# Adding the sparse-attention mask on GpSimd instead of by a TensorE matmul, for five of eight soft-max heads

## The chip, the cores and the metric

The kernel runs on one core of one Trainium2 chip. The metric is the device time of one launch in microseconds (us). The kernel before takes 675.26 us (median of 3 runs, 674.33 to 675.56).

## What is computed

Two layers of an encoder, 512 frames wide 1024. Each layer has one input projection, two kinds of attention on its columns (eight heads each), a gate, an output projection and a layer norm. The change lies in group B, attention over the 128 keys that a cheap indexer picks for each query, with soft-max and a position bias:

```python
score = jnp.where(admissible[None], score, -jnp.inf)
vals, idx = lax.top_k(score, topk)
valid = vals > -jnp.inf
...
logits = jnp.einsum('bqhd,bqkhd->bqhk', qb, kg).astype(jnp.float32) * scale
bias = rel_bias[t5_bucket(idx - t[None, :, None])]
logits = logits + jnp.swapaxes(bias, -1, -2).astype(jnp.float32)
logits = jnp.where(valid[:, :, None, :], logits, -jnp.inf)
p = jax.nn.softmax(logits, axis=-1)
return jnp.einsum('bqhk,bqkhd->bqhd', p.astype(vg.dtype), vg)
```

The kernel gathers nothing. It computes all logits of a block of 128 queries against the keys up to the end of that block and adds a mask: 0 where the key was picked, -1e30 where it was not.

## The kernel before

**Slots.** A layer is a loop over 91 slots (`for s in range(SLOTS + 3)`, L713). Each slot starts one attention block of 128 queries and carries two older ones on. Slots 0 to 23 are the indexer, 24 to 55 the eight stick-breaking heads (class `Stick`), 56 to 87 the eight soft-max heads (class `Soft`, L585). A head is four blocks, `qb` 0 to 3, with n = 128, 256, 384 and 512 keys. Within its slot, a soft-max block does: `stage0` (scores z by TensorE into PSUM), `stage1` (VectorE: negated logits and their row minimum), `stage1b` (ScalarE: exponential and row sum). Two slots later the block is transposed (TensorE, L407) and evacuated (ScalarE L415, VectorE L418); when a head's last block is that far, and one slot more has gone by, `values` multiplies it with the values (TensorE, L556) and `mix` takes the result to M (ScalarE L464, VectorE L466, GpSimd L467).

**Matmul operands** are split in a high and a low part to reach float32 accuracy. So z is two matmuls (L399, L402). Between them stands the mask matmul of a soft-max block:

```python
T.matmul(self.z[:, :nn], a, b, start=True, stop=False)
if mask is not None:
    T.matmul(self.z[:, cols], identb, mask, start=False, stop=False, skip_group_check=True)
T.matmul(self.z[:, :nn], c, d, start=False, stop=True)
```

It multiplies the bf16 mask by a bf16 identity and accumulates it onto z. A stick-breaking block has the same two matmuls and no mask. L599 then adds the position bias: tile `gbias` (512 columns, read backwards), one per head, loaded by `Head.load` (L526) from a table in DRAM into a pool of three buffers.

**Order.** The four compute engines run in the order in which the code issues (`manual_schedule`, L112). The DMA queue of SyncE (SP) isn't in that list: the scheduler places its transfers itself. Between the attention steps of a slot, `fill` issues projection matmuls on TensorE (L221 to L223, L247 to L249) up to a count that the tables `A_PINS`, `B_PINS` and `P1` give for that slot. At the end of a slot, `prep_ahead` (L187) splits the next weight piece: ScalarE writes `whi` (L175) and GpSimd writes `wlo` in two halves of 512 columns (L177). Four `whi`/`wlo` pairs are held at a time.

**GpSimd in the soft-max slots** has the `wlo` splits (L177), one M multiplication per head (L467), one per pair of heads by the reciprocal sums, tile `over` (L550), and from slot 76 on the splits of M for the output projection (L145).

**Pools that the change touches**: `wk` (three buffers, the block tiles `p`, `om` and `relu`) and the two buffers of tile `over` in `tp`.

Of the kernel before, what the change touches and what calls it, by code (L numbers as in the profile page):

```python
# [11 lines left out]
F32 = mybir.dt.float32  # L12
# [3 lines left out]
ALU = mybir.AluOpType  # L16

P = 128
D = 1024
S = 512  # L20
# [11 lines left out]
SCALE = 1.0 / math.sqrt(HD)  # L32
# [59 lines left out]
def tile_hybrid(ctx: ExitStack, tc: tile.TileContext, xt, x, w_in, w_ki, w_out, ln_g, ln_b, rel_bias, onehot, out, depth=DEPTH):  # L92
    nc = tc.nc
    V, A, G, T = nc.vector, nc.scalar, nc.gpsimd, nc.tensor
# [5 lines left out]
    kp = ctx.enter_context(tc.tile_pool(name="kp", bufs=3))  # L100
    vp = ctx.enter_context(tc.tile_pool(name="vp", bufs=2))
    gp = ctx.enter_context(tc.tile_pool(name="gp", bufs=3))
    wk = ctx.enter_context(tc.tile_pool(name="wk", bufs=3))
    tp = ctx.enter_context(tc.tile_pool(name="tp", bufs=2))
    sm = ctx.enter_context(tc.tile_pool(name="sm", bufs=4))
    PS = bass.MemoryType.PSUM
# [12 lines left out]
    mask = [const.tile([P, P * (b + 1)], BF16, name=f"mask{b}") for b in range(NTB)]  # L119
# [89 lines left out]
    def flush():  # L209
        while later:  # L210
            later.pop(0)()
# [67 lines left out]
    def run_pending(at_once=False):  # L279
        for p in pending:  # L280
            p[0] -= 1
        while pending and (at_once or pending[0][0] < 0):
            pending.pop(0)[1]()
# [98 lines left out]
    def load_residual():  # L382
        for tb in range(NTB):
            nc.sync.dma_start(XN[:, tb], x[tb * P : (tb + 1) * P, :])
# [37 lines left out]
    def layer(l):  # L422
        last_layer = l == depth - 1
        st = {}
# [36 lines left out]
        def mix(pair, s, o, engine=G):  # L461
            hi, lo = (slice(0, 64), slice(64, 128)) if s == 0 else (slice(64, 128), slice(0, 64))
            t = tp.tile([P, S], F32, tag="t", name="mixt")
            A.activation(t[hi], o[lo], AF.Copy)  # L464
            if ("g", pair) in made:
                V.tensor_tensor(t[hi], o[hi], t[hi], ALU.add)  # L466
                engine.tensor_tensor(M[hi, pair, :], M[hi, pair, :], t[hi], ALU.mult)  # L467
            else:
                V.tensor_tensor(M[hi, pair, :], o[hi], t[hi], ALU.add)
            made.add(("o", pair, s))  # L470

        def mix_split(pairs, tbs, lo_engine=G):
            src = M[:, pairs, tbs.start * P : tbs.stop * P].rearrange("p m (a b) -> p m a b", b=P)
            hi, lo = (t[:, tbs, pairs, :].rearrange("p a m b -> p m a b") for t in (XH, XL))
            split(hi, lo, src, lo_engine=lo_engine)
# [14 lines left out]
        class Index(Block):  # L490
# [4 lines left out]
            def stage0(self):  # L495
                q = QKV["I", self.h // 4, "q"][self.h % 4 // 2]
                self.product(q, self.h % 2, st["ki"], 0, spare=(3 * self.h + self.qb) % 2 == 0)

            def stage1(self):
                self.r = wk.tile([P, S], F32, tag="w", name="relu")  # L500
                A.activation(self.r[:, : self.n], self.z[:, : self.n], AF.Relu, scale=absw[:, self.qb, self.h : self.h + 1])
# [13 lines left out]
        class Head:  # L515
# [20 lines left out]
            def spread(self):  # L536
                rec = over_sum[self.s]
                V.reciprocal(rec[:, :NTB], self.sums)
                turned = sm.tile([P, 32], F32, tag="turned", name="turned")
                V.transpose(turned, rec)  # L540
                if self.s == 0:
                    st["over"] = tp.tile([P, S], F32, tag="over", name="over")
                rows = r_dram[8 * l + 4 * self.i + self.hh]
                nc.sync.dma_start(rows.rearrange("c (b k) -> b c k", k=32), turned)
                over, pair = st["over"], self.pair
                back = bass.AP(tensor=rows.tensor, offset=rows.offset, ap=[[0, 64], [1, S]])
                part = over[64 * self.s : 64 * self.s + 64]
                pending.append([1, lambda: nc.sync.dma_start(part, back)])
                if self.s == 1:
                    pending.append([SUM_SLOTS, lambda: G.tensor_tensor(M[:, pair, :], M[:, pair, :], over, ALU.mult)])  # L550
# [34 lines left out]
        class Soft(Block):  # L585
            def __init__(self, head, qb):
                super().__init__(qb)
                self.head = head

            def stage0(self):  # L590
                if self.qb == 0:
                    self.head.load()
                self.product(*self.head.operands(), mask=mask[self.qb], cols=slice(0, self.n))

            def stage1(self):
                h, n, b = self.head, self.n, slice(self.qb, self.qb + 1)
                self.p = wk.tile([P, S], F32, tag="w", name="p")
                p = self.p[:, :n]
                V.tensor_tensor_reduce(out=p, in0=self.z[:, :n], in1=h.g[:, :n][:, ::-1], scale=-SCALE, scalar=3.0e38, op0=ALU.add, op1=ALU.min, accum_out=h.mn[:, b])  # L599

            def stage1b(self):
                h, b = self.head, slice(self.qb, self.qb + 1)
# [13 lines left out]
        tasks = [Index(h, qb) for h in range(IDX_HEADS) for qb in range(1, NTB)]  # L616
# [53 lines left out]
        def fill(s):  # L670
            while st["done"] < target(s) - 300:
                if st["gen"] is None:
                    if not queue:
                        return
                    st["gen"] = queue.pop(0)()
                step = next(st["gen"], None)
                if step is None:
                    st["gen"] = None
                else:
                    st["done"] += step  # L680
# [3 lines left out]
        def topk_rounds(upto):  # L684
            while rounds and 48 - len(rounds) < upto:
                qb = rounds.pop(0)
                m8 = sm.tile([P, 8], F32, tag=f"m8{qb}", name="m8", bufs=2)
                V.max(m8, scores[qb])  # L688
                V.match_replace(scores[qb], m8, scores[qb], TAKEN)  # L689
                if not rounds:  # L690
                    for b in range(1, NTB):
                        V.tensor_scalar(mask[b], scores[b], -2.0e38, MASKED, ALU.is_gt, ALU.mult)
# [17 lines left out]
        def at(t):  # L710
            return tasks[t] if 0 <= t < len(tasks) else None

        for s in range(SLOTS + 3):  # L713
            if s == IDX_SLOTS:
                tasks[s - 1].stage2()
                for step in range(PAUSE):
                    fill(s + (step + 1) / PAUSE)
                    flush()
                    topk_rounds(step + 1)
                    stream.prep_ahead()  # L720
            now = s + (s >= IDX_SLOTS)
            done, old = at(s - 3), at(s - 2)
            done = done if isinstance(done, (Stick, Soft)) and done.qb == NTB - 1 else None
            old = old if isinstance(old, (Stick, Soft)) else None
            if at(s):
                tasks[s].stage0()
            if at(s - 1) and s != IDX_SLOTS:
                tasks[s - 1].stage2()
            if at(s):
                tasks[s].stage1()  # L730
            flush()
            fill(now + FRAC[0])
            if old:
                old.transpose()
                old.evacuate(old.head.at)
            if isinstance(at(s), Soft):
                tasks[s].stage1b()
            if old:
                old.evacuate_lo(old.head.at)
            if s in SPLITS:  # L740
                tb = SPLITS.index(s)
                mix_split(slice(0, 6), slice(tb, tb + 1))
            if s == SPLIT6:
                mix_split(slice(6, 7), slice(0, NTB))
            if s >= IDX_SLOTS:
                topk_rounds(PAUSE + RATE * (s + 1 - IDX_SLOTS))
            fill(now + FRAC[1])
            run_pending()
            if done:
                done.head.values()  # L750
                last = s == SLOTS + 2
                mix(done.head.pair, done.head.s, done.head.o, V if last else G)
            fill(now + 1)
            stream.prep_ahead()
            if l == 0 and s == 1:
                load_residual()
                load_bias_table()
            if l == 0 and s in (6, 9):
                make_bias_table(s == 9)
            if s == 72:  # L760
                gb = kp.tile([P, 2, D], F32, tag="k", name="gb")
                for j, t in enumerate((ln_g, ln_b)):
                    row = t[l : l + 1, :]
                    nc.sync.dma_start(gb[:, j, :], bass.AP(tensor=row.tensor, offset=row.offset, ap=[[0, P], [1, D]]))
            if s == PREP[0]:
                stream.prep(index[l, "o"] + 2)
            if s == PREP[1]:
                stream.prep(index[l, "o"] + 3)
# [75 lines left out]
    for l in range(depth):  # L844
        layer(l)
# [49 lines left out]
```

## Time and profile before

| | before |
|---|---|
| Median of 3 runs | 675.26 us (674.33 to 675.56) |
| Profiled execution, its time | 674.73 us |
| Profiled execution, span | 672.9 us |
| TensorE (PE) busy | 659.6 us, 98% |
| PE weight loads (PEld) busy | 553.7 us, 82% |
| VectorE (DVE) busy | 482.7 us, 72% |
| ScalarE (ACT) busy | 351.5 us, 52% |
| GpSimd (POOL) busy | 330.6 us, 49% |
| Mean granted TensorE clock | 0.997 |

A time is some 1.8 us more than the span between the first and the last instruction. Busy times are the union of an engine's instructions. Matmuls overlap in the pipeline, so the duration of one is longer than what it takes from the engine: that is read from one start to the next. Some matmul records are missing from a trace.

### The profile page before, as it was taken

The page shows a single profiled execution, that of the slowest core. Times are in us where ns is not written, and L with a number is a line of the kernel's source. Part 1 is how long each engine was busy: PE and PEld are TensorE (multiplying, and loading weights), DVE is VectorE, ACT ScalarE, POOL GpSimd, SP SyncE. Part 2 cuts the span into 40 slices and gives each one's busy share as a digit, 9 for nine tenths or more (in the row PEclk, how much of TensorE's full clock was granted, in tenths as well). Part 3 has the DMA queues.
Part 4 walks back from the last instruction along what each step waited for, and adds up shares of the span by engine and source line. Part 5 has one row for each costly group of instructions (what it writes and reads, how often), then busy time and mean ns, then how long its engine had stood idle before and what let it go on. Part 6 is the DMA issues. An engine that isn't in the chain of part 4 may idle for free.

```text
span 672.9 us, 10299 instructions
## 1 busy us (share of the span) xinstructions
PE 659.6 (98%) x3575; PEld 553.7 (82%) x3589; DVE 482.7 (72%) x1019; ACT 351.5 (52%) x707; POOL 330.6 (49%) x303
## 2 busy tenths in 40 slices
PE   8999999999999999999999999999999999999995
PEld 4778988988889879877897888889888898897784
DVE  3588899999855455666853689999989554556576
ACT  4576545445447556773233765544534565568610
POOL 5343634466564433764354344445566533457531
PEclk9999999999999999999999999999999999999998
DMA  7625224242342354212125143432114534442022
GB/s 247 221 82 146 95 94 126 64 128 92 99 140 82 115 142 152 82 52 94 41 82 171 64 120 101 126 94 94 64 63 142 126 111 123 123 148 68 32 94 94
DMA packets 26203, 72.85 MB, mean 108 GB/s; under 512 B 5124, under 2 KB 6788, under 8 KB 26152
## 3 DMA queue, kind: packets, MB, share of 16 engines
q1 hardware_dynamic: 26152, 72.20, 34.4%
q8 instruction: 28, 0.46, 0.3%
q14 instruction: 23, 0.19, 0.1%
HBM read 58.87 MB, written 2.31 MB: 91 GB/s over the span
## 4 chain that ended last, share of the span: by engine, by line
PE 88%; DVE 5%; POOL 2%; DMA 2%; issue 1%; ACT 1%; SPq 1%; DVEq 0%; POOLq 0%; ACTq 0%
PE pj L221 14%; PE pj L222 14%; PE pj L223 14%; PE o L556 6%; PE tr L407 5%; PE z L402 4%; PE pjo L642 4%; PE pjo L644 4%; PE pjo L641 4%; PE z L399 4%; PE pjv L249 4%; PE pjv L248 4%; PE pjv L247 4%; POOL wlo L177 1%; DMA XN<-in_xt_dram 1%
## 5 line engine op out<-in xcount | busy, mean ns | idle before, releaser
L177 POOL TENSOR_TENSOR wlo<-raw,whi 128x512 fp32r<-128x512 f32 (+1 forms) x168 | 228.0, 1378 | 157.7 <-ACT whi L175 139.7
L221 PE MATMUL pj<-XH,whi 128*128 128x512 f32 (+1 forms) x456 | 185.4, 407 | 0.4 <-ACT whi L144 0.4
L222 PE MATMUL pj<-XL,whi 128*128 128x512 f32 (+1 forms) x456 | 178.9, 392 | 0.8 <-DVE XL L145 0.8
L223 PE MATMUL pj<-XH,wlo 128*128 128x512 f32 (+1 forms) x456 | 179.2, 393 | 0.0
L223 PEld LDWEIGHTS pj<-XH,wlo 128*128 128x128 f32 (+1 forms) x456 | 84.9, 186 | 20.3 <-POOL wlo L145 0.4
L175 ACT ACTIVATE whi<-raw 128x1024 fp32r<-128x1024 f32 (+1 forms) x87 | 91.2, 1050 | 19.9 <-PE pjo L642 6.6
L222 PEld LDWEIGHTS pj<-XL,whi 128*128 128x128 f32 (+1 forms) x456 | 85.4, 187 | 15.3 <-DVE XL L145 2.4
L221 PEld LDWEIGHTS pj<-XH,whi 128*128 128x128 f32 (+1 forms) x456 | 85.3, 187 | 15.1 <-ACT whi L144 1.1
L247 PE MATMUL pjv<-whi,XH 128*128 128x256 f32 x256 | 75.3, 294 | 0.0
L569 ACT ACTIVATE om<-z 128x128 f32<-128x128 f32 (+1 forms) x64 | 27.9, 437 | 86.9 <-PE z L402 80.7
L575 DVE TENSOR_TENSOR_SCAN om<-om 128x128 f32<-128x128 f32 (+1 forms) x64 | 69.3, 1082 | 5.1 <-POOL om L571 4.9
L249 PE MATMUL pjv<-wlo,XH 128*128 128x256 f32 x256 | 72.5, 283 | 0.3 <-POOL wlo L177 0.3
L248 PE MATMUL pjv<-whi,XL 128*128 128x256 f32 x256 | 72.2, 282 | 0.0
L467 POOL TENSOR_TENSOR M<-M,mixt 64x512 f32<-64x512 f32 x22 | 32.0, 1452 | 72.7 <-DVE mixt L466 39.3
L688 DVE MAX8 m<-scores 128x8 f32<-128x256 f32 (+2 forms) x96 | 52.8, 550 | 0.2
L689 DVE MATCH_REPLACE8 scores<-m,scores 128x256 f32<-128x256 f32 (+2 forms) x96 | 52.1, 542 | 0.0
L641 PE MATMUL pjo<-whi,XH 128*128 128x512 f32 x128 | 51.7, 404 | 0.0
L642 PE MATMUL pjo<-whi,XL 128*128 128x512 f32 x128 | 50.1, 391 | 1.6 <-DVE XL L145 1.6
L418 DVE TENSOR_TENSOR AT<-tr,AT 128x128 fp32r<-128x128 f32 (+1 forms) x64 | 31.3, 490 | 27.9 <-ACT AT L415 27.6
L644 PE MATMUL pjo<-wlo,XH 128*128 128x512 f32 x128 | 50.0, 391 | 0.0
L402 PE MATMUL z<-k,q 128*128 128x256 f32 (+2 forms) x128 | 49.3, 385 | 0.0
L249 PEld LDWEIGHTS pjv<-wlo,XH 128*128 128x128 f32 x256 | 48.6, 190 | 0.7 <-POOL wlo L177 0.7
(125 smaller groups left out, 1192.3 us busy)
## 6 DMA issues: line engine op xcount, KB each, us to landing
raw<-in_w_in_dram SPq DMA_DIRECT2D x70, 512.0 KB, 3.3
k<-k SPq DMA_DIRECT2D x32, 256.0 KB, 5.2
raw<-in_w_out_dram SPq DMA_DIRECT2D x16, 512.0 KB, 3.4
gbias<-f_dram SPq DMA_DIRECT2D x16, 256.0 KB
XN<-in_x_dram SPq DMA_DIRECT2D x4, 512.0 KB
out_dram<-XN SPq DMA_DIRECT2D x8, 256.0 KB, 2.1
M<-M SPq DMA_DIRECT2D x4, 448.0 KB
XN<-in_xt_dram SPq DMA_DIRECT2D x3, 512.0 KB
```

Source lines behind the costliest of these rows:

```text
L175: A.activation(hi[:, :n], raw[:, :n], AF.Copy)
L177: lo_engine.tensor_tensor(lo[:, c], raw[:, c], hi[:, c], ALU.subtract)
L221: T.matmul(o, w[0], XH[:, :, kc, :], start=first, stop=False)
L222: T.matmul(o, w[0], XL[:, :, kc, :], start=False, stop=False)
L223: T.matmul(o, w[1], XH[:, :, kc, :], start=False, stop=last)
L247: T.matmul(acc, XH[:, tb, kc, :], whi, start=kc == 0, stop=False)
L248: T.matmul(acc, XL[:, tb, kc, :], whi, start=False, stop=False)
L249: T.matmul(acc, XH[:, tb, kc, :], wlo, start=False, stop=kc == KC - 1)
L402: T.matmul(self.z[:, :nn], c, d, start=False, stop=True)
L641: T.matmul(acc, XH[:, tb, m, :], whi, start=n == 0, stop=False)
L642: T.matmul(acc, XL[:, tb, m, :], whi, start=False, stop=False)
L644: T.matmul(acc, XH[:, tb, m, :], wlo, start=False, stop=n == 2 * len(mts))
```

## The change

For the first five of a layer's eight soft-max heads (`2 * h.pair + h.s` from 8 to 12) the mask matmul goes. A new step, `prepare`, is issued one slot ahead, right after `stage0` of the slot's own block. It takes the tile `p`, loads the bias at a head's first block, and for these five heads lets GpSimd write bias plus mask into `p` (float32 plus bf16 to float32). VectorE's `stage1` then reads `p` in place of `gbias` and writes over it. The last three heads keep mask matmul and backward read. `wk` gets a fourth buffer, since `p` is now held a slot longer, and `over` has one buffer in place of two.

```diff
-    wk = ctx.enter_context(tc.tile_pool(name="wk", bufs=3))
+    wk = ctx.enter_context(tc.tile_pool(name="wk", bufs=4))
...
-                    st["over"] = tp.tile([P, S], F32, tag="over", name="over")
+                    st["over"] = tp.tile([P, S], F32, tag="over", name="over", bufs=1)
...
+            def prepare(self):
+                h = self.head
+                if self.qb == 0:
+                    h.load()
+                self.p = wk.tile([P, S], F32, tag="w", name="p")
+                self.bias = h.g[:, : self.n][:, ::-1]
+                self.apart = 2 * h.pair + h.s > 12
+                if not self.apart:
+                    G.tensor_tensor(self.p[:, : self.n], self.bias, mask[self.qb], ALU.add)
+                    self.bias = self.p[:, : self.n]
+
             def stage0(self):
-                if self.qb == 0:
-                    self.head.load()
-                self.product(*self.head.operands(), mask=mask[self.qb], cols=slice(0, self.n))
+                self.product(*self.head.operands(), mask=mask[self.qb] if self.apart else None, cols=slice(0, self.n))

             def stage1(self):
                 h, n, b = self.head, self.n, slice(self.qb, self.qb + 1)
-                self.p = wk.tile([P, S], F32, tag="w", name="p")
                 p = self.p[:, :n]
-                V.tensor_tensor_reduce(out=p, in0=self.z[:, :n], in1=h.g[:, :n][:, ::-1], scale=-SCALE, scalar=3.0e38, op0=ALU.add, op1=ALU.min, accum_out=h.mn[:, b])
+                V.tensor_tensor_reduce(out=p, in0=self.z[:, :n], in1=self.bias, scale=-SCALE, scalar=3.0e38, op0=ALU.add, op1=ALU.min, accum_out=h.mn[:, b])
...
             if at(s):
                 tasks[s].stage0()
+            if isinstance(at(s + 1), Soft):
+                tasks[s + 1].prepare()
             if at(s - 1) and s != IDX_SLOTS:
                 tasks[s - 1].stage2()
```

In the rows below the lines of the changed kernel are its own: its L599 is the GpSimd add, and what was L599 on VectorE is L608.

On TensorE, this is the first soft-max block of layer 0, with fill matmuls around it (identb is the bf16 identity, mask_109 the mask of the first query block):

```order
 L249 MATMUL pjv<-wlo_2151,XH 128x256
 L399 MATMUL z<-k,q 128x256
-L401 LDWEIGHTS identb
-L401 MATMUL z<-mask_109,identb 128x128
 L402 MATMUL z<-k,q 128x256
 L247 MATMUL pjv<-whi_2150,XH 128x256
```

A weight load and a matmul are gone; the rows around them stand as they stood. The same happens at 40 blocks, and nothing else of TensorE's order changes.

On GpSimd, this is the queue of the kernel before from the last stick-breaking block (L571) to the M multiplication after the second soft-max head's third block (layer 0):

```order
L571 AFFINE_SELECT om<-om 128x128
L177 TENSOR_TENSOR wlo_2328<-raw_2155,whi_2327 128x512 x2
L467 TENSOR_TENSOR M<-M,mixt 64x512
L177 TENSOR_TENSOR wlo_2382<-raw_2214,whi_2381 128x512 x2
L177 TENSOR_TENSOR wlo_2497<-raw_2332,whi_2496 128x512 x2
```

And the same place in the changed kernel:

```order
L599 TENSOR_TENSOR p<-gbias,mask_109 128x128
L571 AFFINE_SELECT om<-om 128x128
L599 TENSOR_TENSOR p<-gbias,mask_110 128x256
L599 TENSOR_TENSOR p<-gbias,mask_111 128x384
L177 TENSOR_TENSOR wlo_2330<-raw_2155,whi_2329 128x512 x2
L599 TENSOR_TENSOR p<-gbias,mask_112 128x512
L467 TENSOR_TENSOR M<-M,mixt 64x512
L177 TENSOR_TENSOR wlo_2384<-raw_2214,whi_2383 128x512 x2
L599 TENSOR_TENSOR p<-gbias,mask_109 128x128
L599 TENSOR_TENSOR p<-gbias,mask_110 128x256
L599 TENSOR_TENSOR p<-gbias,mask_111 128x384
L177 TENSOR_TENSOR wlo_2499<-raw_2334,whi_2498 128x512 x2
```

The adds stand between the old instructions, which keep their order. The first head's first add stands ahead of the last L571; the second head's first add (the second mask_109) stands behind a `wlo` pair.

On SP, this is the piece around the bias load of the sixth head of layer 0 (k<-k are copies of a key tile to the other half of the partitions):

```order
 L148 DMA k<-k 64x1024 x2
 L548 DMA over<-r_dram 64x512
+L530 DMA gbias<-f_dram 128x512
 L148 DMA k<-k 64x1024 x2
-L163 DMA raw_2686<-in_w_out_dram 128x1024
-L530 DMA gbias<-f_dram 128x512
+L163 DMA raw_2688<-in_w_out_dram 128x1024
 L544 DMA r_dram<-turned 4x32x32
```

The bias load moves ahead of two key copies and one weight load. The next head's moves ahead of two loads of layer-norm rows in the same way; nothing else on SP changes places.

## Rows read from the trace of the kernel before

**Rows 1.** Busy time by engine: stretch, PE, PEld, DVE, ACT, POOL, PEclk, DMA share, GB/s

```profile
208.00:273.00 65.00, 65.00 (x422) 57.23 (x427) 35.50 (x103) 41.37 (x100) 26.96 (x22) 1.00 0.41 127
```

**Rows 2.** Waits of TensorE, whole span: us in total, times, longest us

```profile
PE pjo L642 <- DVE XL L145: 1.6, 2, 0.8
...
PE o L556 <- DVE AT L418: 0.5, 2, 0.2
```

**Rows 3.** Line L401, the mask matmul's weight loads: duration ns min/median/max, starts, forms

```profile
L401 PEld LDWEIGHTS <-identb x64: 95/95/99, 208.2 to 625.5; 128*128 128x128 bf16 x64
```

**Rows 4.** Timeline of PE, second soft-max head, layer 0: start us, us, instruction

```profile
220.25 0.28 PE L399 MATMUL z<-k,q 128*128 128x256 f32 x1
...
220.61 0.27 PE L247 MATMUL pjv<-whi,XH 128*128 128x256 f32 x1
...
223.07 0.28 PE L399 MATMUL z<-k,q 128*128 128x256 f32 x1
...
223.44 0.27 PE L247 MATMUL pjv<-whi,XH 128*128 128x256 f32 x1
...
226.32 0.33 PE L399 MATMUL z<-k,q 128*128 128x384 f32 x1
...
226.84 0.27 PE L407 MATMUL tr<-ident,p 128*128 128x128 f32 x1
...
230.31 0.39 PE L399 MATMUL z<-k,q 128*128 128x512 f32 x1
...
230.99 0.39 PE L221 MATMUL pj<-XH,whi 128*128 128x512 f32 x1
```

**Rows 5.** Timeline of PE, stick-breaking blocks of layer 0, which have no mask

```profile
108.87 0.33 PE L399 MATMUL z<-k,q 128*128 128x384 f32 x1
...
109.21 0.40 PE L221 MATMUL pj<-XH,whi 128*128 128x512 f32 x1
...
114.07 0.39 PE L399 MATMUL z<-k,q 128*128 128x512 f32 x1
...
114.52 0.39 PE L221 MATMUL pj<-XH,whi 128*128 128x512 f32 x1
...
118.19 0.28 PE L399 MATMUL z<-k,q 128*128 128x256 f32 x1
...
118.43 0.40 PE L221 MATMUL pj<-XH,whi 128*128 128x512 f32 x1
```

**Rows 6.** POOL by line and form, 208 to 273 us: count, busy us, mean ns, idle before

```profile
L177 POOL TENSOR_TENSOR wlo<-raw,whi 128x512 fp32r<-128x512 f32 x16 | 20.3, 1291 | 17.3 <-ACT whi L175 15.3 <-DMA gbias<-f_dram 1.7
```

**Rows 7.** POOL by line and form, whole span, the widest two-input form

```profile
L145 POOL TENSOR_TENSOR XL<-M,XH 128x768 fp32r<-128x768 f32 x8 | 14.6, 1839 | 6.8 <-ACT XH L144 6.8
```

**Rows 8.** POOL by line and form, stick-breaking heads, 60 to 208 us

```profile
L177 POOL TENSOR_TENSOR wlo<-raw,whi 128x512 fp32r<-128x512 f32 x44 | 63.4, 1462 | 33.4 <-ACT whi L175 33.3
```

**Rows 9.** Timeline of POOL, soft-max heads of layer 0

```profile
219.50 2.54 POOL L177 TENSOR_TENSOR wlo<-raw,whi 128x512 fp32r<-128x512 f32 x2
...
234.22 2.54 POOL L177 TENSOR_TENSOR wlo<-raw,whi 128x512 fp32r<-128x512 f32 x2 [1.74 <-DMA gbias<-f_dram]
...
264.20 2.54 POOL L177 TENSOR_TENSOR wlo<-raw,whi 128x512 fp32r<-128x512 f32 x2 [2.91 <-ACT whi L175]
```

**Rows 10.** Timeline of DVE: L599 of two blocks, and the L466 after the second

```profile
220.81 0.29 DVE L599 CUSTOM_DVE_ANT_0 p<-z,gbias 128x128 f32<-128x128 f32 x1 [0.31 <-PE z L402]
...
266.49 0.56 DVE L599 CUSTOM_DVE_ANT_0 p<-z,gbias 128x384 f32<-128x384 f32 x1 [0.63 <-PE z L402]
...
269.29 0.69 DVE L466 TENSOR_TENSOR mixt<-o,mixt 64x512 f32<-64x512 f32 x1 [1.63 <-ACT mixt L464]
```

**Rows 11.** Timeline of ACT: end of the exponential of the second head's first block

```profile
222.16 0.19 ACT L604 ACTIVATION_READ_ACCUMULATOR p<-p,mn 128x1 f32 x1
```

**Rows 12.** Timeline of SP's queue, layer 0

```profile
219.16 0.33 SPq L530 DMA_DIRECT2D gbias<-f_dram  x1
...
242.44 1.23 SPq L148 DMA_DIRECT2D k<-k  x2
```

## The prediction

> **What bounds the kernel now.** I read the share of busy time first, then the stretch that the change touches, then the waits. Over the span TensorE is busy 98%, but an average hides stages, so the stretch of layer 0 that holds the five changed heads (208 to 273 us) counts: there TensorE is busy 65.00 us of 65.00 at a granted clock of 1.00, while VectorE has 35.50, ScalarE 41.37 and GpSimd 26.96 [rows 1]. The reader is to see that only one engine is full, and that GpSimd has more idle than busy time. A full engine can still be waiting inside; the table of waits excludes it: the longest wait of TensorE's matmuls in the whole execution comes to 1.6 us over two times, and the only one in the soft-max heads is 0.5 us over two times, values matmuls waiting for an evacuated tile [rows 2]. So in these heads TensorE's own work sets the end. What is taken from it shortens the time, as long as nobody else becomes late enough to stop it.
>
> **What leaves TensorE.** The mask is one weight load and one matmul in each of 64 blocks [rows 3]; 40 of them go (5 heads, 4 blocks, 2 layers). The printed duration of a matmul is no price, because matmuls overlap; starts are. From the first z matmul to the first instruction after the second, a soft-max head takes 0.36, 0.37, 0.52 and 0.68 us in its four blocks [rows 4]. The same pair without a mask, in stick-breaking blocks of the same shapes, takes 0.24, 0.34 and 0.45 us; the 128-key block also computes 256 columns, so 0.24 holds for the first two [rows 5]. The differences are 0.12, 0.13, 0.18 and 0.23 us, together 0.66 us a head. Ten heads make **6.6 us**. Readings go in steps of 0.01 us, so a difference may be off by 0.02, and 40 of them by 0.8 us.
>
> The Trainium skill (TensorE: Matmul & The Clock Gate, section Back-to-back issue gap) gives a matmul of N columns at the full clock N/2.4 + 2.5 ns. By it the four mask matmuls would be worth 0.54 us a head and the change 5.4 us, an estimate from that page. The rows show more, and they decide.
>
> Why more is plain from the rows: a weight load of 95 ns belongs to each mask [rows 3], and the 128-key mask costs as much as the 256-key one [rows 4].
>
> **What GpSimd gets.** 40 adds, each of two inputs. The trace has no GpSimd add with a bf16 input or a backward read, so the price comes from float32 neighbours: 1291 ns for 512 columns in the very stretch [rows 6] and 1839 ns for 768 [rows 7]. That is 2.14 ns a column and 195 ns fixed: 0.47, 0.74, 1.02 and 1.29 us for the four blocks, 3.52 us a head, 17.6 us a layer. From below, with nothing fixed, 2.52 ns a column of the first row gives 3.2 us a head; from above, the 512-column form at its mean of 1462 ns among the stick-breaking heads [rows 8] gives 4.0. I take 3.52, because its rows run beside the same neighbours. A layer's stretch then holds 27.0 + 17.6 = 44.6 us of GpSimd work in 61.7 us (65.0 less 3.3), 72%. It fits; this costs nothing of itself.
>
> **What waits for the adds.** GpSimd runs in order, so an add behind a pair of weight splits comes when these are done. The worst place is the second head's first block. The splits end at 219.50 + 2.54 = 222.04, the add at 222.51; VectorE began this block's L599 at 220.81 [rows 9, 10]. So VectorE is held 1.7 us, and behind it in its queue an evacuation of the head before. The exponential ended at 222.35 [rows 11], and TensorE transposes the block at 226.84 [rows 4]: 4.5 us spare, 2.8 left. The third head's splits at 234.22 [rows 9] stand behind its first add, and don't hold it.
>
> The second place is the third block of the fifth head: the splits end at 266.74 [rows 9], the add of 1.02 us at 267.76, against a start of 266.49 [rows 10]: 1.3 us late. Next in line is L466, the first step to M; it had been idle 1.63 us for ScalarE [rows 10], so 1.3 us are swallowed, with 0.3 us left. By the same sum no other add is as late. I cost these waits at nothing. Their cover is that spare time; if it is gone, TensorE waits for the remainder.
>
> **What else moves.** The bias loads are no new wait: the load at 219.16 [rows 12] is the layer's fourth, issued as the second head begins, since three buffers exist, and the buffer now comes free when GpSimd has read it, a slot earlier. One bias load moves ahead of key copies on SP, which were issued at 242.44 [rows 12]. It waits for the third head's last add. That add stands third behind the splits that end at 236.76 [rows 9], so by 236.76 + 0.74 + 1.02 + 1.29 = 239.8: no delay. Cover gone, the key copies would be as late as that add; those keys serve a later head. The weight pieces come later by an add at most, 1.3 us, with four pairs held. The single buffer of `over` is read a slot or more before the next pair's sums are fetched. VectorE's L608 has the same sizes as L599, and the fourth `wk` buffer can only remove waits: nothing for both. The first head's first add (0.47 us) delays the mask of the last stick-breaking block, and so its scan; that block too is transposed two slots later.
>
> **Sum.** 674.73 (profiled) less 6.6 is 668.1 us. The profiled execution lies 0.5 us below the median shown, so the median becomes 675.26 - 6.6 = **668.7 us**.
>
> **The rivals.** *Late adds reach TensorE, in part.* The fifth head's late add passes L466, the M multiplication, and the splits of M to ScalarE and the values matmuls that already wait [rows 2]. If L466's spare is not there, because with TensorE faster its input comes sooner, 1.3 us a layer come back: 668.7 + 2.6 = 671.3 us. For it: there is a wait of this kind already. Against: all of these steps follow TensorE, and move forward with it.
>
> *Nothing is won.* Both late places get through in full, 1.7 + 1.3 us a layer, 6.0 us in all: 674.7 us, within 0.2% of the time before (1.35 us, about what a measurement can tell from no change). Against: 2.8 us spare at the first.
>
> *GpSimd becomes the bound, and the kernel slower.* The one price without a row is the bf16, backward add. The stretch has 65.0 - 27.0 = 38.0 us for adds before a layer takes longer than now; that is 2.16 times 17.6. From there each further microsecond of adds comes out at the end, through VectorE waiting, the exponential, and transposes that find no tile. At 2.5 times, 27.0 + 44.0 = 71.0 us, 6.0 over in each layer: 687 us. For it: no row prices these operands. Against: the widest spread that one shape shows is 1462 against 1291 ns [rows 6, 8], a factor of 1.13.
>
> A rule of the Trainium skill (SBUF — State Buffer, section Who interferes with whom) speaks for a dearer add: a VectorE instruction with two SBUF inputs contends with a GpSimd one that reads SBUF. In these heads VectorE's L608 and the evacuations have one input in PSUM, so by this rule the price stays; the lower mean among soft-max heads agrees [rows 6, 8]. By it alone, where it did strike, the factor would stay at 1.13 here.
>
> That the change doesn't do what it says is excluded: the order shows 80 TensorE instructions fewer and 40 GpSimd adds more.
>
> **How the numbers follow.** Forecast 0.73: every row on the path bears it, and the cover is measured. Late adds in part 0.13, nothing won 0.06, slower 0.08. Faster by over 0.2% is 0.73 + 0.13 = 0.86, no change 0.06, slower 0.08. The range starts at 668.7 less 0.8 for the readings less 0.9 for the spread of runs (675.26 to 674.33), 667.0. It reaches to the partial rival, 671.3, and 0.7 for the same errors: 672.0. Left out are the last two rivals, 0.14.
>
> **What would show it.** Right: 24 weight loads at L401 in place of 64; the four spacings at 0.24, 0.24, 0.34 and 0.45 in the changed heads; GpSimd busy about 35 us more; TensorE still full in the stretch, which is 3.3 us shorter in each layer; VectorE waiting for GpSimd once or twice a layer, below 2 us each. Wrong: an add of 512 columns well over 1.5 us; TensorE waiting for `p` at its transposes, or for `AT` at the values by more than 0.5 us in all; a stretch that shortens while another grows.

## The result, and the profile after

The changed kernel takes **671.24 us** (median of 4 runs, 670.55 to 671.97) against 675.03 us for the kernel before (4 runs): a ratio of 0.9945, 95% interval 0.9927 to 0.9962. It is faster by 3.8 us, inside the range and 2.5 us above the forecast of 668.7. The profiled execution took 671.17 us, its span is 669.4 against 672.9 us, 3.5 us less.

The removal itself is as forecast. This is line L401 in the trace of the changed kernel (duration in ns, min/median/max; starts; forms):

```profile
L401 PEld LDWEIGHTS <-identb x24: 95/96/98, 268.8 to 622.0; 128*128 128x128 bf16 x24
```

And this the timeline of TensorE for the blocks that [rows 4] show before: start and duration in us.

```profile
220.03 0.28 PE L399 MATMUL z<-k,q 128*128 128x256 f32 x1
...
220.27 0.28 PE L247 MATMUL pjv<-whi,XH 128*128 128x256 f32 x1
...
225.90 0.33 PE L399 MATMUL z<-k,q 128*128 128x384 f32 x1
...
226.24 0.27 PE L407 MATMUL tr<-ident,p 128*128 128x128 f32 x1
...
229.72 0.39 PE L399 MATMUL z<-k,q 128*128 128x512 f32 x1
...
230.17 0.39 PE L221 MATMUL pj<-XH,whi 128*128 128x512 f32 x1
```

The spacings are 0.24, 0.34 and 0.45 us, those of [rows 5]. GpSimd's adds are a little cheaper than taken (0.47, 0.74, 1.02 and 1.29 us); whole span, by form, with busy us and mean ns of one:

```profile
L599 POOL TENSOR_TENSOR p<-gbias,mask 128x512 f32<-128x512 f32 x10 | 11.8, 1178 | 0.0
L599 POOL TENSOR_TENSOR p<-gbias,mask 128x384 f32<-128x384 f32 x10 | 9.7, 974 | 0.4 <-PE tr L407 0.4
L599 POOL TENSOR_TENSOR p<-gbias,mask 128x256 f32<-128x256 f32 x10 | 6.8, 679 | 0.0
L599 POOL TENSOR_TENSOR p<-gbias,mask 128x128 f32<-128x128 f32 x10 | 4.3, 426 | 0.0
```

What came in exchange stands in the waits of TensorE (us in total, times, longest):

```profile
PE o L556 <- ACT AT L415: 2.2, 2, 1.2
PE pjo L651 <- DVE XL L145: 1.6, 2, 0.8
PE pj L222 <- DVE XL L145: 1.2, 2, 0.9
...
PE tr L407 <- DVE om L575: 0.9, 3, 0.5
PE o L556 <- DVE AT L418: 0.5, 2, 0.2
```

The table of the kernel before has no row like the first, and the fourth row here holds one new wait of 0.45 us. VectorE waited for the adds in both layers; the same table says of its L608:

```profile
DVE p L608 <- POOL p L599: 11.1, 8, 2.4
```

So more adds came late than the two that the prediction named. Most of this was swallowed before it reached TensorE.

**Where the time went**, by subtracting the starts of the same z matmuls in both traces. Ahead of the first changed block the changed kernel is 0.39 us late (the loads at its start landed later). Through the five heads of layer 0 it comes to 2.81 us early: a gain of 3.20. Three blocks on, at the fourth block of the sixth head, it is 1.92 early: 0.89 lost. Layer 1 begins 1.97 early, loses 0.65 between the first head's second and third block, and reaches 4.57 early after five heads, so its gain is 3.25; the same fourth block costs 1.09. That is 6.45 us gained, 2.63 lost, 0.39 not the change's: 3.43 us, of 3.5 in the spans.

**The larger loss**, followed back in layer 0. TensorE, then ScalarE, VectorE and GpSimd, each as its own timeline of the changed kernel (the bracket is the idle time before and what ended it):

```profile
274.78 0.49 PE L556 MATMUL o<-AT,vt 128*128 128x512 f32 x1 [1.00 <-ACT AT L415]
275.51 1.34 PE L556 MATMUL o<-AT,vt 128*128 128x512 f32 x7 [0.23 <-DVE AT L418]
```

```profile
266.01 0.62 ACT L613 ACTIVATE p<-p,mn 128x384 f32<-128x384 f32 x1 [1.72 <-DVE mn L608]
266.54 0.19 ACT L613 ACTIVATION_READ_ACCUMULATOR p<-p,mn 128x1 f32 x1
266.75 0.59 ACT L464 ACTIVATE mixt<-o 64x512 f32<-64x512 f32 x1
...
273.40 0.84 ACT L144 ACTIVATE XH<-M 128x768 fp32r<-128x768 f32 x1 [2.44 <-POOL M L550]
274.15 0.58 ACT L415 ACTIVATE AT<-tr 128x512 fp32r<-128x512 f32 x1
```

```profile
265.35 0.56 DVE L608 CUSTOM_DVE_ANT_0 p<-z,p 128x384 f32<-128x384 f32 x1 [1.91 <-POOL p L599]
...
267.37 0.69 DVE L466 TENSOR_TENSOR mixt<-o,mixt 64x512 f32<-64x512 f32 x1 [0.85 <-ACT mixt L464]
```

```profile
261.90 2.53 POOL L177 TENSOR_TENSOR wlo<-raw,whi 128x512 fp32r<-128x512 f32 x2 [1.52 <-ACT whi L175]
264.39 2.06 POOL L599 TENSOR_TENSOR p<-gbias,mask 128x384 f32<-128x384 f32 x2
268.21 1.29 POOL L467 TENSOR_TENSOR M<-M,mixt 64x512 f32<-64x512 f32 x1 [1.75 <-DVE mixt L466]
269.58 2.55 POOL L177 TENSOR_TENSOR wlo<-raw,whi 128x512 fp32r<-128x512 f32 x2
272.08 1.29 POOL L550 TENSOR_TENSOR M<-M,over 128x512 f32<-128x512 f32 x1
```

Read from below. The add of the fifth head's third block stands behind a pair of splits and begins at 264.39 (its row also holds the next add, of 512 columns). VectorE waits 1.91 us for it; before, it had been idle 0.63 us ahead of this block [rows 10], so the add makes it 1.3 us late. ScalarE's exponential waits for VectorE, and behind it in ScalarE's queue stands L464, the copy of the fourth head's values. Its matmuls began at 264.53, and it begins 2.22 us after them. In the kernel before it began 1.56 us after them and waited for these matmuls alone (ScalarE's timeline before):

```profile
268.67 0.59 ACT L464 ACTIVATE mixt<-o 64x512 f32<-64x512 f32 x1 [0.81 <-PE o L556]
```

So 0.66 us of the 1.3 get through to L464. Everything after keeps its distances: M multiplication, splits, multiplication by the sums, then ScalarE's split of M, and behind that the evacuation for which the fifth head's values matmuls wait. (The expectations below call these the sixth head's values; they are issued in that head's third slot.)

**The smaller loss** is a scan in layer 1, on VectorE, then TensorE, then GpSimd:

```profile
536.58 2.58 DVE L575 TENSOR_TENSOR_SCAN om<-om 128x512 f32<-128x512 f32 x1 [0.40 <-POOL om L571]
```

```profile
539.30 0.63 PE L407 MATMUL tr<-ident,om 128*128 128x128 f32 x4 [0.45 <-DVE om L575]
```

```profile
535.87 0.43 POOL L599 TENSOR_TENSOR p<-gbias,mask 128x128 f32<-128x128 f32 x1
536.25 0.29 POOL L571 TENSOR_SCALAR_AFFINE_SELECT om<-om 128x128 f32<-128x128 f32 x1
536.51 1.56 POOL L599 TENSOR_TENSOR p<-gbias,mask 128x256 f32<-128x256 f32 x2
```

The scan of the last stick-breaking block begins 0.4 us late and takes 2.58 us, beside two adds (the last row holds the one of 256 columns and the one of 384). The same scan took 1.22 us before:

```profile
538.10 1.22 DVE L575 TENSOR_TENSOR_SCAN om<-om 128x512 f32<-128x512 f32 x1
```

In layer 0 the scan took 1.70 us and TensorE lost nothing. There GpSimd waited for a transpose ahead of the 384-column add, the scan got in first, and the add took 1.39 us in place of 0.93:

```profile
209.63 1.39 POOL L599 TENSOR_TENSOR p<-gbias,mask 128x384 f32<-128x384 f32 x1 [0.42 <-PE tr L407]
```

### The profile page after: what moved, and what is told of

The parts are those of the page before. It is cut to its first block, busy times and chain, and to the rows that moved or that the text cites. A ratio compares the mean times of both kernels' runs of the same rounds, so it can differ in the third digit from the quotient of the medians.

```text
span 669.4 us, 10343 instructions
## 1 busy us (share of the span) xinstructions
PE 653.1 (98%) x3549; PEld 551.8 (82%) x3549; DVE 483.1 (72%) x1019; ACT 351.8 (53%) x707; POOL 362.0 (54%) x343
## 4 chain that ended last, share of the span: by engine, by line
PE 84%; DVE 5%; POOL 4%; issue 2%; ACT 2%; DMA 2%; SPq 1%; DVEq 0%; POOLq 0%; ACTq 0%
PE pj L221 14%; PE pj L223 14%; PE pj L222 14%; PE o L556 5%; PE tr L407 5%; PE pjo L651 4%; PE pjo L653 4%; PE pjo L650 4%; PE z L399 4%; PE z L402 4%; PE pjv L249 4%; PE pjv L248 3%; PE pjv L247 3%; POOL wlo L177 3%; DVE om L575 1%
## 5 line engine op out<-in xcount | busy, mean ns | idle before, releaser
L575 DVE TENSOR_TENSOR_SCAN om<-om 128x128 f32<-128x128 f32 (+1 forms) x64 | 71.2, 1113 | 5.8 <-POOL om L571 5.6
L571 POOL TENSOR_SCALAR_AFFINE_SELECT om<-om 128x128 f32<-128x128 f32 x64 | 23.0, 361 | 52.4 <-ACT om L569 46.4
L556 PE MATMUL o<-AT,vt 128*128 128x256 f32 (+2 forms) x256 | 47.8, 327 | 2.7 <-ACT AT L415 2.2
```

The source lines that it names most:

```text
L556: T.matmul(self.o[:, q0 * P :], vt[:, sb, self.hh * P : (self.hh + 1) * P], at_block(self.at[j], sb, q0, NTB - q0), start=n == 0, stop=n == 7)
L575: V.tensor_tensor_scan(rev, rev, rev, 1.0, ALU.mult, ALU.min)
```

## The experiments

Two theories for the larger loss stood against each other. A: the late add goes through ScalarE's queue to the values. B: TensorE, now faster, arrives earlier at a chain that was full already, and the late add is swallowed. For the scan: order (C) or mutual hindrance of VectorE and GpSimd (D).

**No mask at all in the five heads.**

```diff
-                if not self.apart:
-                    G.tensor_tensor(self.p[:, : self.n], self.bias, mask[self.qb], ALU.add)
-                    self.bias = self.p[:, : self.n]
```

> The mask is left out for the five heads of each layer: neither matmul nor GpSimd add (so the softmax there runs over all computed keys; the pools are the change's). It is the change at a price of nothing for the adds. Theory A (what is missing from the forecast 6.6 us is due to the adds: a wait at the sixth head's values in each layer, and a late scan in layer 1): the TensorE spacings give 3.2 us a layer; the waits for the values fall from 1.2 us to about 0.6 each (0.34 us because TensorE arrives earlier, 0.23 us as before), the scan's wait of layer 1 goes; 669.2 us. Rival B (the adds cost nothing; the time is lost because TensorE arrives earlier at a chain that doesn't move with it): about the change's own time, 671.2 us, and waits of 1.2 us at the values.

Measured 669.01 us (ratio 0.9906, 0.9892 to 0.9919). The wait at the values, TensorE's timeline:

```profile
273.87 0.50 PE L556 MATMUL o<-AT,vt 128*128 128x512 f32 x1 [0.32 <-ACT AT L415]
```

In layer 1 it is 0.31 us, the scan takes 1.23 us, nothing waits for it. By the starts, the sixth head's fourth block costs 0.20 us a layer. So of 0.89 and 1.09 us some 0.2 are B's and the rest is due to the adds, as A has it; with the scan the adds cost 2.2 us in all.

**The adds ahead of the weight splits**, five heads as in the change.

```diff
+        held = []
...
+            if held:
+                held.clear()
+                stream.prep_ahead()
...
-            stream.prep_ahead()
+            soon = at(s + 2)
+            if isinstance(soon, Soft) and 2 * soon.head.pair + soon.head.s <= 12:
+                held.append(1)
+            else:
+                stream.prep_ahead()
```

(The list stands ahead of the loop over the slots, the second piece behind the call of `prepare`, the third at the end of the slot.)

> The same five heads and adds; only the weight split at the end of a slot is issued a little later, behind the add of the next slot, so that no add stands behind a pair of splits on GpSimd. Theory A (the fifth head's third add is late behind a pair, VectorE waits 1.9 us, ScalarE's exponential with it, and the copy of the values' result behind that): that wait of VectorE falls below 0.5 us, the wait for the values of the sixth head from 1.2 to about 0.6 us in each layer, the time by 1.3 us to 669.9. Rival B (TensorE arrives earlier, the late add is swallowed): the add is on time, the wait stays at 1.2 us and the time at 671.2. A third outcome: the splits become late, and TensorE waits for wlo.

Measured 669.86 us (0.9922, 0.9908 to 0.9935). No wait of VectorE for an add is left, and the values wait as without adds:

```profile
274.38 0.50 PE L556 MATMUL o<-AT,vt 128*128 128x512 f32 x1 [0.32 <-ACT AT L415]
```

By the starts, the sixth head's fourth block costs 0.20 us in each layer, as without adds. Splits later by an add stopped nobody. A holds, in path and size.

**The late add twice.**

```diff
+                    if 2 * h.pair + h.s == 12 and self.qb == 2:
+                        G.tensor_tensor(self.p[:, : self.n], self.bias, mask[self.qb], ALU.add)
```

> The change, with the late add of the fifth head's third block done twice (the second writes the same sums again). Theory A: the copy of the values' result comes later by the whole add of 1.0 us, and so does the wait for the values: from 1.2 to 2.2 us in each layer, 673.2 us. If the late add were swallowed on the way, the wait would stay near 1.2 us.

Measured 674.66 us, in a single execution. The waits at the values, TensorE's timeline:

```profile
275.82 0.49 PE L556 MATMUL o<-AT,vt 128*128 128x512 f32 x1 [1.98 <-ACT AT L415]
...
606.39 0.49 PE L556 MATMUL o<-AT,vt 128*128 128x512 f32 x1 [2.19 <-ACT AT L415]
```

One microsecond more of add is one microsecond more of wait (1.00 and 1.20 in the change). The rest of the miss, 1.5 us, lies in layer 0 just behind the wait: the next head's first block comes that much later, and the granted clock, 1.00 in the change, is below it (busy time by engine, 5 us each, PEclk, DMA share, GB/s):

```profile
275.00:280.00 5.00, 3.95 (x14) 2.90 (x16) 3.08 (x9) 4.22 (x12) 2.39 (x2) 0.76 0.27 98
280.00:285.00 5.00, 5.00 (x28) 4.09 (x27) 2.51 (x12) 3.88 (x12) 5.00 (x4) 0.90 0.12 34
285.00:290.00 5.00, 5.00 (x28) 3.98 (x27) 3.09 (x10) 3.67 (x11) 2.98 (x3) 1.00 0.28 101
```

The mean of 0.76 is part of the time at 1.2 GHz. Behind layer 1's wait of 2.19 us the granted clock stayed at 1.00, and nothing more was lost.

**One multiplication by the sums a slot earlier.**

```diff
-                    pending.append([SUM_SLOTS, lambda: G.tensor_tensor(M[:, pair, :], M[:, pair, :], over, ALU.mult)])
+                    pending.append([SUM_SLOTS - (pair == 5), lambda: G.tensor_tensor(M[:, pair, :], M[:, pair, :], over, ALU.mult)])
```

> The change, with one multiplication moved: for the second pair of soft-max heads M times the reciprocal sums is issued one slot sooner on GpSimd, ahead of the pair of splits that it stood behind. If the chain that ends at the sixth head's values goes through this multiplication (ScalarE's split of M waits for it, and holds ScalarE's queue, and the evacuation behind it), the wait of 1.2 us in each layer goes altogether: 2.4 us, 668.8 us. If the late add reaches the values on another way (through VectorE's queue), the wait stays above 0.6 us and the time above 670. GpSimd may wait up to 1.5 us for the sums' transfer; that costs nothing under both.

Measured 669.52 us (0.9908, 0.9895 to 0.9922). That is 1.7 us of the 2.4 that were expected. In layer 0 the wait for ScalarE is gone; in layer 1 it stays:

```profile
601.20 0.50 PE L556 MATMUL o<-AT,vt 128*128 128x512 f32 x1 [0.96 <-ACT AT L415]
```

GpSimd's timeline says why:

```profile
269.29 1.30 POOL L550 TENSOR_TENSOR M<-M,over 128x512 f32<-128x512 f32 x1 [2.94 <-DMA over<-r_dram]
...
597.13 1.28 POOL L550 TENSOR_TENSOR M<-M,over 128x512 f32<-128x512 f32 x1 [4.01 <-DVE mn L608]
```

GpSimd stood idle 2.9 and 4.0 us (I allowed 1.5), and the M multiplication behind was held up with it. In layer 0 the row names the sums' transfer; in layer 1 it names an instruction of VectorE long done, so the transfer is likely there too, but the trace doesn't show it. The chain does go through this multiplication: in layer 0 all of the loss went. Issued a slot earlier it meets the sums' transfer, and in layer 1 the chain is hardly shorter.

**The first add behind the last stick-breaking mask.**

```diff
-            if isinstance(at(s + 1), Soft):
+            first = isinstance(at(s), Stick) and isinstance(at(s + 1), Soft)
+            if isinstance(at(s + 1), Soft) and not first:
                 tasks[s + 1].prepare()
...
             if at(s):
                 tasks[s].stage1()
+            if first:
+                tasks[s + 1].prepare()
```

> The change, with the first head's first add issued behind the mask of the last stick-breaking block instead of ahead of it. In the change the scan of that block in layer 1 took 2.58 us instead of 1.22 and began late, and TensorE waited 0.45 us. Theory C (order: the add of 0.43 us ahead delays the scan): the scan begins 0.4 us sooner and TensorE no longer waits. Rival D (VectorE's scan and GpSimd's adds hold each other up while they run side by side): the scan in layer 1 still takes about 2.5 us, the adds beside it are longer than their like, and a wait of 0.2 us or more stays.

Measured 670.17 us, in a single execution. The scan in layer 1 and the add of 256 columns beside it, VectorE's timeline, then GpSimd's:

```profile
536.04 1.45 DVE L575 TENSOR_TENSOR_SCAN om<-om 128x512 f32<-128x512 f32 x1
```

```profile
536.36 1.59 POOL L599 TENSOR_TENSOR p<-gbias,mask 128x256 f32<-128x256 f32 x1
```

The scan begins without a wait and TensorE no longer waits for it, as C said. But it isn't as short as without adds (1.45 against 1.23 us), and the add beside it is longer than its like (1.59 against 0.67 us in the change), as D said; D's 2.5 us of scan and its wait did not come. C and D both act, one through the other: the order decides which adds are ahead of the scan. Here that is the 128-column add, which ends at 536.40; in the change it was the 256-column one in layer 0 (until 209.21) and the 256- and 384-column ones in turn in layer 1 (until 538.08). In all three cases the scan ends 1.1 us after that, at 537.49, 210.30 and 539.16. Its row begins beside an add, but it ends about its own length (1.22 us) after the adds ahead of it. With this scan mended, the wait for the values in layer 1 is 0.99 us as in layer 0, so the 0.2 us that layer 1 lost more there went with it too.

**Both orders mended.** The edits of the two runs together.

> The change with both orders mended: weight splits issued behind the next slot's add, and the first head's first add behind the mask of the last stick-breaking block. If the two late adds are all that the adds cost, this is the run without mask and adds in time: 0.3 us of wait for the values in each layer on top of the 0.2 us that was there before, none for the scan, 669.0 us. If GpSimd's work costs something else too, it is slower than that run by more than 0.5 us.

Measured 669.11 us (0.9911, 0.9897 to 0.9924), the time without mask and adds to 0.1 us, where the interval of each is 0.9 us to either side; by the starts both gain 6.0 us from the first soft-max block on. Waits 0.33 us at the values, none at the scan. The late third block and the first head's first add are all that the adds cost.

**The held pair of splits**, on top of both orders.

```diff
             run_pending()
+            if s == 75:
+                stream.prep_ahead()
...
-            else:
+            elif s != 74:
                 stream.prep_ahead()
```

> The kernel with both orders mended, and one pair of weight splits (and its ScalarE copy) held back to the next slot, behind the multiplication of M by the reciprocal sums of the second pair of heads. If what is left of the wait for the values (0.3 and 0.2 us a layer) is the chain M multiplication, splits of 2.5 us, multiplication by the sums, ScalarE's split of M, evacuation, it goes in both layers: 1.1 us, 667.9 us. If the sums' transfer lands late, or the later weight piece stops TensorE, the wait stays or another takes its place, and the time is 669 or more.

Measured **667.12 us** (0.9878, 0.9865 to 0.9892), the best here. The values matmuls run through in both layers; layer 0:

```profile
273.81 1.54 PE L556 MATMUL o<-AT,vt 128*128 128x512 f32 x8
```

It is 0.8 us better than expected.

**The hold alone**, on the kernel before (the same edit, without the adds).

> The kernel before, with only the pair of weight splits held back behind the multiplication by the sums; all masks on TensorE, no GpSimd adds. It removes the wait of 0.23 us a layer at the fifth head's values: 0.5 us, 674.7 us against 675.2. If the hold was worth as much without the adds as with them (2.0 us), that part of the best version has nothing to do with the mask, and this kernel takes 673.2.

Measured 673.61 us (0.9982, 0.9973 to 0.9991), nearer to the second outcome. By the starts of the z matmuls it gains 0.87 us in each layer, not 0.23: of what the kernel before lost at this place, the wait of 0.23 us [rows 2] shows a quarter. Most of the rest shows only in starts. From the transpose ahead to the first values matmul it went from 0.37 to 0.03 us, and from the first values matmul to the second from 0.73 to 0.31. So some 1.5 of the 2.0 us that the held pair gained with the adds have nothing to do with the mask.

**All eight heads** and **six heads**, both with mended orders and the held pair. The edits are the limit in `prepare` (15 and 13 in place of 12) and, with eight, the slots in which the splits stand behind the add.

```diff
-                self.apart = 2 * h.pair + h.s > 12
+                self.apart = 2 * h.pair + h.s > 15
...
-            if isinstance(soon, Soft) and 2 * soon.head.pair + soon.head.s <= 12:
+            if isinstance(soon, Soft) and s + 2 <= 75:
```

> The kernel before, with all eight heads on GpSimd: three more heads lose the mask matmul. By the TensorE spacings this is worth 0.64 us a head, 3.9 us: 664.0 us if GpSimd carries it. In the last three heads GpSimd was busy some 64% of the time, and 10 us of adds in 24 us of stretch leave it almost none idle: I expect late adds, VectorE waiting for them, and waits of TensorE for p or AT that give back a part: 664 to 667 us. Above 668 us GpSimd is the bound there.

> The kernel with mended orders and the held pair of splits, with six heads on GpSimd in place of five. By the spacings the sixth head is worth 0.64 us a layer: 665.8 us if its adds come in time. With all eight, TensorE waited 1.2 and 1.3 us at the fifth head's values, while the sixth head ran; if that came from the sixth head's own adds, standing before and behind the held pair and ahead of the splits of M, it shows here too and the kernel is slower than with five heads, 669 us or more. If it came from the heads behind, it is gone here.

Eight heads: 680.19 us, slower than the kernel before (1.0073, 1.0059 to 1.0087). Six heads: 673.45 us (0.9971, 0.9959 to 0.9982), 6.3 us worse than five. The six-head kernel shows it with one head; GpSimd, VectorE and TensorE, each its own timeline:

```profile
271.03 2.55 POOL L177 TENSOR_TENSOR wlo<-raw,whi 128x512 fp32r<-128x512 f32 x2
273.54 0.68 POOL L599 TENSOR_TENSOR p<-gbias,mask 128x256 f32<-128x256 f32 x1
```

```profile
274.25 0.42 DVE L608 CUSTOM_DVE_ANT_0 p<-z,p 128x256 f32<-128x256 f32 x1 [2.48 <-POOL p L599]
...
274.60 0.69 DVE L418 TENSOR_TENSOR AT<-tr,AT 128x512 fp32r<-128x512 f32 x1
```

```profile
275.34 1.08 PE L556 MATMUL o<-AT,vt 128*128 128x512 f32 x5 [1.26 <-DVE AT L418]
277.73 0.50 PE L556 MATMUL o<-AT,vt 128*128 128x256 f32 x2 [1.30 <-DVE vt L291]
```

The sixth head's second add stands behind the held pair; VectorE waits 2.48 us with the evacuation behind it, TensorE twice. The waits come from that head's own adds, as the first half of the expectation had it. By the starts they cost 2.0 us in each layer, and in layer 1 the next head is another 1.4 us late at a granted clock of 0.66 over 5 us. Six heads without the held pair, or with the pair behind that add, were not tried.

Eight heads are 13 us above the upper end of my estimate (664 to 667). I had counted busy time, not where the adds stand. GpSimd isn't full even there: in layer 0 it is busy 19.7 of 24.0 us from 273 to 297 us, while TensorE waits for late tiles and its granted clock is 0.86. How the loss divides between late adds and the clock stays open.

**The pools alone**, on the kernel before: `wk` with four buffers, `over` with one.

> The kernel before with the change's pools alone: four buffers for the block tiles, one for the reciprocal sums. Forecast in the prediction at nothing: 675.2 us, within 0.2% of the kernel before, and the same TensorE spacings. If the fourth buffer removes waits on the path, or the one buffer makes one, it is off by more.

Measured 674.95 us against 675.10 (0.9998, 0.9989 to 1.0007). Nothing, and the starts of the z matmuls keep a constant distance of 0.3 us from the kernel before's through both layers.

## Why the prediction was right, and where it was not

**What bounds the kernel: right.** With the matmuls gone TensorE moved forward by their spacing. But the prediction took the only wait in these heads at its 0.5 us; by the starts of the hold alone, 1.7 us were lost there in the two layers.

**What leaves TensorE: right.** 6.6 us forecast, 6.45 by the starts. The 5.4 us that the prediction worked out from the Trainium skill (TensorE: Matmul & The Clock Gate, section Back-to-back issue gap) were too few. That the weight load makes up the difference is likely, but no run takes it out by itself.

**What GpSimd gets: right.** 3.52 us a head forecast, 3.26 measured, so no extra cost of the bf16 input and the backward read shows. The rival in which dearer adds make GpSimd the bound was wrong. With eight heads the kernel did become slower, but not by dearer adds: there they take 1.18 us for 512 columns as with five, and stand late in the queue. The sentence that contention would leave the factor at 1.13 was wrong where contention struck: beside the last scan one add took 1.39 in place of 0.93 us, and another 1.59 in place of 0.67.

**What waits for the adds: here the forecast failed.** The step reads: "Next in line is L466, the first step to M; it had been idle 1.63 us for ScalarE [rows 10], so 1.3 us are swallowed, with 0.3 us left." The lateness was right (VectorE idle 1.91 us where it had been idle 0.63). But L466's idle time was a wait for ScalarE, and ScalarE was itself behind VectorE: its exponential waits for L608, and the copy L464 that feeds L466 stands behind the exponential. Spare time on one engine is no cover when the engine that it waits for is held by the same delay. So 0.7 us of the 1.3 came through to the values, in place of none.

The rival of late adds, 671.3 us, named the right place and the right chain behind it, and by this mechanism its chance of 0.13 was too low. That its time is the measured one to 0.1 us is partly luck. It took 2.6 us from the late add; the late add cost 1.4 us in the two layers, TensorE's earlier arrival 0.4, and the scan, which the rival doesn't have, the rest. Its reason, that L466's input comes sooner because TensorE is faster, is not what happened: that input came later, through ScalarE's queue. And the reason against it, that these steps "move forward" with TensorE, holds but for the 0.2 us a layer of earlier arrival.

The other named late place, the second head's first block, was swallowed as forecast. So was one that the prediction didn't name, the fourth head's first block: VectorE waited 1.6 us for its add in each layer, where it had been idle 0.9.

**The first head's first add: wrong.** I took 0.47 us of delay for the scan, with two slots to spare. The delay was 0.40 us, but the two adds ahead made the scan 1.36 us longer in layer 1, and 0.65 us were lost. The rule of the Trainium skill that I set beside the slow rival (SBUF — State Buffer, section Who interferes with whom) was the right rule: a VectorE instruction with two SBUF inputs contends with a GpSimd one that reads SBUF. The traces agree with it: 1.23 us without adds, 1.45 beside the short one, 2.58 beside the two longer ones in layer 1. I held it against L608 and the evacuations and didn't ask which of the adds runs beside the last scan, which reads `om` twice. The trace of the kernel before could have answered: its 16 scans of this shape take from 1.21 to 3.49 us, and the longest runs beside a pair of splits (VectorE, then GpSimd):

```profile
168.71 3.49 DVE L575 TENSOR_TENSOR_SCAN om<-om 128x512 f32<-128x512 f32 x1
```

```profile
168.59 2.53 POOL L177 TENSOR_TENSOR wlo<-raw,whi 128x512 fp32r<-128x512 f32 x2
```

The pair ends at 171.12 and the scan 1.1 us later, at 172.20.

**What else moves: right.** The pools do nothing, no bias load was late, and splits later by an add stopped nobody.

**The end**: 668.7 forecast, 671.24 measured. The likeliest case was the wrong one; the range held because it reached to the rival of late adds. One step of the range doesn't come out: the "same errors" are 0.7 us at its upper end and 1.7 at its lower. By the prediction's own signs the outcome is mixed: the weight loads and spacings are those of "right", but TensorE waited 2.7 us for `AT` at the values, where more than 0.5 in all was a sign of "wrong", and VectorE waited for GpSimd more often and longer (up to 2.4 us) than once or twice below 2.

## What to carry to other kernels

When work moves to an engine that is half idle, its busy share says little: find, for each new instruction, what stands ahead of it in that in-order queue, and move it ahead of the long pair that can wait. Spare time must be followed through every engine on the path, since an idle time that ends on another engine vanishes when the same delay holds that engine. Then look for the chain that the saved time runs into: here one pair of splits issued a slot later was worth another 2.0 us, 1.5 of them also in the kernel without the adds.

## What the runs showed of the hardware that was not expected

A scan on VectorE whose two inputs are one SBUF tile took 1.23 us with GpSimd idle, 1.45 us beside a 128-column GpSimd add, 1.70 us beside a 256-column one (layer 0) and 2.58 us beside a 256- and a 384-column one in turn (layer 1). An add that begins behind the start of such a scan is held as well: 1.59 us in place of 0.67 for 256 columns.

A TensorE wait can cost more than its length: around and behind a wait of 1.98 us the granted clock was 0.76 and 0.90 in two stretches of 5 us, and 1.5 us were lost on top; behind one of 2.19 us in the same execution it stayed at 1.00.

And it can be longer than its row: a wait listed at 0.23 us gave back 0.87 us when it was removed.
